# Modulation rows turned into columns: fp32 products with a vector of ones, or one-pass transposes and a VectorE sum

## The chip, the cores and the metric

The kernel runs on one core of a Trainium2 chip. Its time is the device time of one execution in microseconds (us). The kernel before took 1846.21 us (median of three runs, 1843.55 to 1846.67).

## The reference

Two layers, each a token mixer (layer 0: chunked gated linear attention, GLA; layer 1: an S5 state-space layer) around a residual stream of 256 tokens by 2048 features, everything in fp32. Ahead of each mixer the input is modulated by shift and scale vectors that a conditioning vector `c` gives:

```
mod = silu(c) @ ada_w + ada_b                      # per layer: 2048 -> 3 * 2048
for i in range(2):
    shift, scale, gate = split(mod[i], 3)          # 2048 each
    u = x * (1 + scale) + shift
    h = gla_mixer(u, ...) if i == 0 else s5_mixer(u, ...)
    x = layer_norm(alpha * x + (1 + gate) * h, ln_g[i], ln_b[i])
```

Only the way in which `shift` and `scale` get from the sums of products to the place where `u` is made is touched here.

## The kernel before

**Layout.** The mixers take `u` transposed: features on the 128 partitions, tokens along the free axis, in 16 blocks of 128 features. So `shift` and `scale` are wanted as columns: a tile `mods` of 128 partitions by (layer, part, block), part 0 the shift, part 1 one plus the scale. The products `silu(c) @ ada_w`, though, are gathered as rows: a tile of 128 partitions by up to 512 output features, in which each partition holds the part of the sum that its rows of `ada_w` gave, so that the total is still to be summed over the partitions. `mod_cols` does both steps at once: for each block of 128 features it multiplies the row block (as the stationary operand) with one column of ones, and the result is a column of 128 totals. VectorE then adds the bias `abT` (and 1.0 for the scale) and writes `mods`.

**Who makes the rows.** Layer 0's rows come from `ada_pe`, either by TensorE into a PSUM tile `psa` that ScalarE copies to `row` (L275, L278), or, with `dve=True`, by VectorE multiply-adds into `row` (L265, L267). Layer 1's come from `ada_dve`, by VectorE multiply-adds into `acc` (L311, L315), 512 features at a time. In all `mod_cols` is called 18 times: for layer 0 four times with two blocks and six times with four, for layer 1 eight times with four: 64 blocks in all. In the profile its products are line L236 (tile `psmod`), the bias adds L239 (shift) and L241 (scale).

**The work around it.** The weights of the big products stream in by DMA, 128 x 1024 at a time (`wload`, L136, issued by SyncE's queue); `split` makes of each a rounded part on ScalarE (`hi...`, L145) and a remainder on VectorE (`lo...`, L146), and TensorE multiplies with both (L167 to L169 for the v products and the output projection, L180 to L182 for q, k and z). `u` itself is made block by block: TensorE transposes x (`u_tr`, L363, tile `psx`), VectorE applies scale and shift (`u_fin`, L370, tile `uf`), and ScalarE and VectorE split that too (L351, L352). VectorE also adds the v products to `vbig` (L401) and scales the q and k products into `qk` (L415).

**Order.** Layer 0's modulation runs among the first 60 weight steps: a table (`put_ada`, `put_u`) says at which step a load, a product or the columns are put, and `issue_after` ties them to that step's last split and last matmul. Layer 1's steps wait in a list `bg` from which `pump` takes some at each weight step. Within these ties a scheduler sets each engine's order; every engine runs its own list in order. PSUM tiles of `mod_cols` come from the pool `ax` of three.

Of the kernel before, what the change touches and what calls it, by code (L numbers as in the profile page):

```python
# [8 lines left out]
F32 = mybir.dt.float32  # L9
F32R = mybir.dt.float32r  # L10
AF = mybir.ActivationFunctionType
ALU = mybir.AluOpType
# [3 lines left out]
P = 128  # L16
# [17 lines left out]
def trunk(ctx, tc, x, c, ln_g, ln_b, ada_w, ada_b, gla_w_in, gla_gate_w2, gla_gate_b, gla_norm_g,  # L34
# [3 lines left out]
    V, S, PE = nc.vector, nc.scalar, nc.tensor  # L38
# [3 lines left out]
    def pool(name, bufs=1, **kw):  # L42
        return ctx.enter_context(tc.tile_pool(name=name, bufs=bufs, **kw))

    cp = pool("const")
# [23 lines left out]
    ones = rp.tile([P, P], F32, tag="ones", name="ones0")  # L69
# [10 lines left out]
    def psx(name):  # L80
        return ax.tile([P, 512], F32, tag="ax", name=name)

    ident = cp.tile([P, P], F32, name="ident")
# [139 lines left out]
    ps = psx("psc")  # L223
# [6 lines left out]
    mods = cp.tile([P, 2, 2, 16], F32, name="mods")  # L230

    def mod_cols(row, l, part, k0, nk):

        ps = psx(f"psmod{l}{part}{k0}")
        for i in range(nk):
            PE.matmul(ps[:, i:i + 1], lhsT=row[:, i * P:(i + 1) * P], rhs=ones[:, 0:1], start=True, stop=True)  # L236
        ab = abT[:, 32 * l + 16 * part + k0:32 * l + 16 * part + k0 + nk]
        if part == 0:
            V.tensor_tensor(mods[:, l, 0, k0:k0 + nk], ps[:, 0:nk], ab, op=ALU.add)  # L239
        else:  # L240
            V.scalar_tensor_tensor(mods[:, l, 1, k0:k0 + nk], ps[:, 0:nk], 1.0, ab, op0=ALU.add, op1=ALU.add)  # L241

    def ada_pe(l, part, k0, nk, dve=False, rows=None):

# [37 lines left out]
        if dve:  # L282
            steps = [lambda kq=kq, h=h: madds(kq, h) for kq in range(len(rows)) for h in range(2)]
        return [lambda kq=kq: load(kq) for kq in range(len(rows))], steps, lambda: mod_cols(acc[0], l, part, k0, nk)

    def ada_now(*a, rows=None, between=None):
# [11 lines left out]
    def ada_dve(l, part, j):  # L298
# [18 lines left out]
        def fin():  # L317
            if part < 2:
                mod_cols(acc[0], l, part, 4 * j, 4)
            else:  # L320
                br = rp.tile([1, 512], F32, tag="br", name=f"br{l}{j}", bufs=1)
                dma(br, ada_b[l:l + 1, 2 * D + j * 512:2 * D + (j + 1) * 512])
                ps = psx(f"psg{l}{j}")
                V.tensor_tensor(acc[0][0:1, :], acc[0][0:1, :], br, op=ALU.add)
                if l:
                    ah = tp.tile([P, 512], F32R, tag="ah", name=f"ah{j}", bufs=1)
                    al = tp.tile([P, 512], F32R, tag="al", name=f"al{j}", bufs=1)
                    hilo(ah, al, acc[0])
                    PE.matmul(ps, lhsT=ones_r, rhs=ah, start=True, stop=False)
                    PE.matmul(ps, lhsT=ones_r, rhs=al, start=False, stop=True)  # L330
                else:
                    PE.matmul(ps, lhsT=ones, rhs=acc[0], start=True, stop=True)
                if gate_dst[l] is None:
                    gate_dst[l] = s8t(f"gate{l}", [D])
                S.activation(gate_dst[l][:, j * 512:(j + 1) * 512], ps, AF.Identity, bias=ones[:, 0:1])
# [111 lines left out]
    ps = psx("psv2")  # L447
# [395 lines left out]
    for h in range(4):  # L843
        ps = psx(f"psst{h}")
        for cc, (r, a, b) in enumerate(((0, 0, 256), (64, 64, 256), (0, 256, 384), (64, 320, 384))):
            for t in range(2):
                PE.matmul(ps[r:r + 64, a:b], lhsT=kt[:, 2 * h + t, cc * 64:cc * 64 + 64], rhs=qs[cc][:, 2 * h + t, :],
                          start=(t == 0), stop=(t == 1))
# [62 lines left out]
    for g in range(8):  # L911
# [9 lines left out]
        for f in range(4):  # L921
            i = (g * 4 + f) % 8
# [103 lines left out]
    for k in range(16):  # L1026
        ps = psx(f"psn{k}")
# [242 lines left out]
    for g in range(8):  # L1270
# [7 lines left out]
        for f in range(4):  # L1278
            i = (g * 4 + f) % 8
# [27 lines left out]
    ones = rp.tile([P, P], F32, tag="ones", name="ones1")  # L1307
# [14 lines left out]
    for g in range(8):  # L1322
# [17 lines left out]
        for f in range(4):  # L1340
            i = g * 4 + f
# [78 lines left out]
    ps = psx("psnb")  # L1420
    PE.transpose(ps[:2, 0:P], nbs, ident)
    row = tp.tile([2, P], F32, tag="row2", name="row2", bufs=1)
# [31 lines left out]
```

## Time and profile before

| | |
|---|---|
| median of three runs | 1846.21 us (1843.55 to 1846.67) |
| profiled execution, own time | 1847.81 us |
| its span on the core | 1846.0 us |
| mean granted TensorE clock | 0.989 |
| TensorE busy | 1795.7 us, 97% |
| VectorE busy | 1401.8 us, 76% |
| ScalarE busy | 895.7 us, 49% |
| products of `mod_cols` (L236) | 128 records, 12.2 us to 752.5 us after the start |
| VectorE idle ahead of the bias adds (L239, L241) | 16.8 us and 12.9 us |

The profile is of one execution; its span is the time from the first to the last record, and the execution's own time is 1.8 us more. A record is one instruction as the engine ran it. PE is TensorE's matmuls, PEld its weight loads, DVE VectorE, ACT ScalarE, SPq SyncE's queue. In rows of the timeline the first number is the start in us, the second the duration; in brackets stands how long the engine had been idle, and what ended that.

### The profile page before, as it was taken

To read this page: it belongs to the slowest core of one execution; us is meant where nothing else is said; L and a number is where in the kernel's file an instruction comes from. 1 tells how busy PE (TensorE), PEld (TensorE's weight loads), DVE (VectorE), ACT (ScalarE), POOL (GpSimd) and SP (SyncE) were. 2 spreads that over 40 slices of the span, in tenths; PEclk is the share of its full clock that TensorE was granted. 3 is DMA by queue.
4 is the path that set the end of the run, shared out by engine and by line. 5 is a ranking of instruction groups with operands and counts; after the bars stand their busy time and mean duration, and the time that the engine had idled before them with its cause. 6 is when DMAs were issued, how large, how long until landed. Compare 5 with 4: busy or idle time off the path is not lost.

```text
span 1846.0 us, 33780 instructions
## 1 busy us (share of the span) xinstructions
PE 1795.7 (97%) x13555; PEld 1587.8 (86%) x13555; DVE 1401.8 (76%) x1862; ACT 895.7 (49%) x1266; POOL 85.6 (5%) x94
## 2 busy tenths in 40 slices
PE   7999999999999999999999999999999999999997
PEld 5776897899999888799998989989888888888885
DVE  4877667879989988686799779888677775557556
ACT  4432557555556333554454444545544544444332
POOL 0000000000000000002232300000000000000000
PEclk9999999999999999999999999999999999999998
DMA  9996885889889998577666567899788886668653
GB/s 342 380 325 226 293 263 165 262 270 322 290 277 324 331 356 287 171 248 212 197 175 196 173 194 219 232 254 240 220 276 267 270 277 209 190 192 325 193 183 92
DMA packets 246101, 457.86 MB, mean 248 GB/s; under 512 B 19828, under 2 KB 49198, under 8 KB 244662
## 3 DMA queue, kind: packets, MB, share of 16 engines
q1 hardware_dynamic: 239320, 436.02, 73.8%
q0 software_dynamic: 5856, 18.63, 3.1%
q8 instruction: 106, 1.74, 0.4%
q10 hardware_dynamic: 768, 1.05, 0.2%
q14 instruction: 51, 0.42, 0.1%
HBM read 437.01 MB, written 18.61 MB: 247 GB/s over the span
## 4 chain that ended last, share of the span: by engine, by line
PE 83%; DVE 9%; DMA 3%; issue 2%; ACT 2%; POOL 0%; SPq 0%; DVEq 0%; ACTq 0%; POOLq 0%
PE gl L192 13%; PE gl L193 7%; PE op L168 6%; PE op L167 6%; PE op L169 6%; PE z L182 3%; PE z L180 3%; PE z L181 3%; PE v L168 3%; PE v L169 3%; PE v L167 3%; PE su L180 2%; PE su L181 2%; PE su L182 2%; PE sz L180 2%
## 5 line engine op out<-in xcount | busy, mean ns | idle before, releaser
L146 DVE TENSOR_TENSOR logl<-wgl,higl 128x1024 fp32r<-128x1024 f32 x128 | 156.6, 1223 | 115.7 <-ACT higl L145 109.2
L145 ACT CAST higl<-wgl 128x1024 fp32r<-128x1024 f32 x128 | 134.4, 1050 | 170.7 <-PE gl L192 163.0
L192 PE MATMUL gl<-yp,higl 128*128 128x512 f32 x512 | 179.3, 395 | 0.1
L192 PE MATMUL gl<-yb,higl 128*128 128x512 f32 x512 | 179.1, 395 | 0.0
L145 ACT CAST hio<-wo 128x1024 fp32r<-128x1024 f32 x95 | 100.2, 1055 | 154.7 <-PE op L169 134.4
L146 DVE TENSOR_TENSOR loo<-wo,hio 128x1024 fp32r<-128x1024 f32 x95 | 116.1, 1223 | 67.1 <-ACT hio L145 66.6
L315 DVE SCALAR_TENSOR_TENSOR acc<-wa,cs,acc 128x512 f32<-128x512 f32 x217 | 162.1, 747 | 4.0 <-DMA wa<-in_ada_w 1.1
L180 PE MATMUL sz<-u1h,hisz 128*128 128x256 f32 x512 | 151.0, 295 | 1.3 <-ACT zs L1282 1.2
L180 PE MATMUL su<-u1h,hisu 128*128 128x256 f32 x512 | 151.8, 298 | 0.0
L180 PE MATMUL z<-u0h,hiz 128*128 128x256 f32 x512 | 148.7, 290 | 0.0
L182 PE MATMUL sz<-u1h,losz 128*128 128x256 f32 x512 | 145.6, 285 | 3.1 <-DVE losz L146 3.1
L182 PE MATMUL su<-u1h,losu 128*128 128x256 f32 x512 | 146.7, 287 | 0.0
L181 PE MATMUL su<-u1l,hisu 128*128 128x256 f32 x512 | 146.4, 286 | 0.0
L182 PE MATMUL z<-u0h,loz 128*128 128x256 f32 x512 | 144.9, 283 | 0.6 <-DVE loz L146 0.6
L181 PE MATMUL sz<-u1l,hisz 128*128 128x256 f32 x512 | 145.4, 284 | 0.0
L181 PE MATMUL z<-u0l,hiz 128*128 128x256 f32 x512 | 144.7, 283 | 0.0
L193 PE MATMUL gl<-yb,logl 128*128 128x256 f32 x512 | 142.9, 279 | 0.0
L193 PE MATMUL gl<-yp,logl 128*128 128x256 f32 x512 | 142.2, 279 | 0.0
L145 ACT CAST hisz<-wsz 128x1024 fp32r<-128x1024 f32 x64 | 67.0, 1050 | 117.7 <-PE sz L181 62.0
L192 PEld LDWEIGHTS gl<-yp,higl 128*128 128x128 f32 x512 | 95.9, 188 | 22.8 <-issue 0.7
L192 PEld LDWEIGHTS gl<-yb,higl 128*128 128x128 f32 x512 | 96.0, 188 | 22.6
L168 PE MATMUL v<-lov,u0h 128*128 128x512 f32 x256 | 103.6, 406 | 6.9 <-DVE lov L146 6.8
(321 smaller groups left out, 4974.0 us busy)
## 6 DMA issues: line engine op xcount, KB each, us to landing
wgl<-in_s_w_glu SPq DMA_DIRECT2D x128, 512.0 KB, 4.5
wa<-in_ada_w SPq DMA_DIRECT2D x116, 512.0 KB, 5.3
wv<-in_gla_w_in SPq DMA_DIRECT2D x64, 512.0 KB, 5.8
wz<-in_gla_w_in SPq DMA_DIRECT2D x64, 512.0 KB, 5.1
wsu<-in_s_w_in SPq DMA_DIRECT2D x64, 512.0 KB, 4.3
wsz<-in_s_w_in SPq DMA_DIRECT2D x64, 512.0 KB, 5.7
wo<-in_s_w_out SPq DMA_DIRECT2D x64, 512.0 KB, 4.6
a<-in_ada_w SPq DMA_DIRECT2D x31, 1024.0 KB, 10.8
```

The source lines that it names most:

```text
L145: S.copy(hi, w)
L146: last_lo[0] = V.tensor_tensor(lo, w, hi.bitcast(F32), op=ALU.subtract).ins
L167: PE.matmul(banks[tt], lhsT=uh, rhs=hi[:, kk, :], start=(k == first), stop=False)
L168: PE.matmul(banks[tt], lhsT=uh, rhs=lo[:, kk, :], start=False, stop=False)
L169: last_mm[0] = PE.matmul(banks[tt], lhsT=ul, rhs=hi[:, kk, :], start=False, stop=(k == last)).ins
L180: PE.matmul(o, lhsT=wh, rhs=u.hi(k), start=(k == first), stop=False)
L181: PE.matmul(o, lhsT=wh, rhs=u.lo(k), start=False, stop=False)
L182: last_mm[0] = PE.matmul(o, lhsT=wl, rhs=u.hi(k), start=False, stop=(k == last)).ins
L192: PE.matmul(banks[f], lhsT=hi[:, kk, fs], rhs=u.both(k), start=(k == 0), stop=False)
L193: PE.matmul(banks[f][:, :T], lhsT=lo[:, kk, fs], rhs=u.hi(k), start=False, stop=(k == last))
L315: V.scalar_tensor_tensor(acc[0], w[:, kk, :], cs[:, k:k + 1], acc[0], op0=ALU.mult, op1=ALU.add)
```

## The change

`mod_cols` no longer multiplies with ones. It transposes each row block on TensorE, into a PSUM tile of 128 x (blocks x 128) in which partition p holds, for each block, the 128 addends of feature p; VectorE sums them along the free axis into a small tile `modsum`; the bias adds then read `modsum` in place of PSUM.

```
     ps = psx(f"psmod{l}{part}{k0}")
     for i in range(nk):
-        PE.matmul(ps[:, i:i + 1], lhsT=row[:, i * P:(i + 1) * P], rhs=ones[:, 0:1], start=True, stop=True)
+        PE.transpose(ps[:, i * P:(i + 1) * P], row[:, i * P:(i + 1) * P], ident)
+    sm = cp.tile([P, 4], F32, tag="modsum", name=f"modsum{l}{part}{k0}", bufs=2)[:, :nk]
+    V.tensor_reduce(sm, ps[:, :nk * P].rearrange("p (i q) -> p i q", i=nk), op=ALU.add, axis=mybir.AxisListType.X)
     ab = abT[:, 32 * l + 16 * part + k0:32 * l + 16 * part + k0 + nk]
     if part == 0:
-        V.tensor_tensor(mods[:, l, 0, k0:k0 + nk], ps[:, 0:nk], ab, op=ALU.add)
+        V.tensor_tensor(mods[:, l, 0, k0:k0 + nk], sm, ab, op=ALU.add)
     else:
-        V.scalar_tensor_tensor(mods[:, l, 1, k0:k0 + nk], ps[:, 0:nk], 1.0, ab, op0=ALU.add, op1=ALU.add)
+        V.scalar_tensor_tensor(mods[:, l, 1, k0:k0 + nk], sm, 1.0, ab, op0=ALU.add, op1=ALU.add)
```

All later line numbers grow by two. TensorE's instructions stay as many, apart from one group of layer 1 that the scheduler now splits in one and three; VectorE's grow by 18. The scheduler also moves some neighbours. Two places matter for what follows, both on VectorE in layer 0; names carry the buffer's number, and what is the same tile has a number greater by 10 to 12 in the changed kernel.

VectorE about 83 us after the start, before, at the scale of blocks 4 to 7 (`vbig` is the running sum of the v products, `lov` the remainder of the next weights, which TensorE needs):

```order
L267 SCALAR_TENSOR_TENSOR row_527<-a_525,cs,row_527 128x512
L401 TENSOR_TENSOR vbig<-vbig,v_761 128x512
L241 SCALAR_TENSOR_TENSOR mods<-psmod_751,abT 128x4
L401 TENSOR_TENSOR vbig<-vbig,v_762 128x512
L146 TENSOR_TENSOR lov_788<-wv_651,hiv_787 128x1024
L146 TENSOR_TENSOR lov_819<-wv_677,hiv_818 128x1024
L401 TENSOR_TENSOR vbig<-vbig,v_785 128x512
```

The same place in the changed kernel:

```order
L269 SCALAR_TENSOR_TENSOR row_535<-a_533,cs,row_535 128x512
L403 TENSOR_TENSOR vbig<-vbig,v_771 128x512
L146 TENSOR_TENSOR lov_798<-wv_659,hiv_797 128x1024
L238 TENSOR_REDUCE modsum_764<-psmod_759 128x4
L403 TENSOR_TENSOR vbig<-vbig,v_772 128x512
L243 SCALAR_TENSOR_TENSOR mods<-modsum_764,abT 128x4
L146 TENSOR_TENSOR lov_829<-wv_685,hiv_828 128x1024
L403 TENSOR_TENSOR vbig<-vbig,v_795 128x512
```

The first `lov` has moved ahead of everything that waits for `psmod`; the reduce and the bias add stand behind it, with a `vbig` between them.

VectorE about 101 us after the start, before, at the shift of blocks 4 to 7 (`loq` is the remainder of the next q weights, `uf` the modulated input, from which the next stationary blocks are made):

```order
L415 SCALAR_TENSOR_TENSOR qk_115<-q_934,qk_115 128x256
L146 TENSOR_TENSOR loq_992<-wq_783,hiq_991 128x1024
L239 TENSOR_TENSOR mods<-psmod_924,abT 128x4
L415 SCALAR_TENSOR_TENSOR qk_115<-q_935,qk_115 128x256
L415 SCALAR_TENSOR_TENSOR qk_115<-q_936,qk_115 128x256
L415 SCALAR_TENSOR_TENSOR qk_115<-q_937,qk_115 128x256
L370 TENSOR_SCALAR uf_975<-psx_970,mods 128x256
```

The same place in the changed kernel:

```order
L417 SCALAR_TENSOR_TENSOR qk_115<-q_946,qk_115 128x256
L238 TENSOR_REDUCE modsum_939<-psmod_934 128x4
L146 TENSOR_TENSOR loq_1004<-wq_793,hiq_1003 128x1024
L241 TENSOR_TENSOR mods<-modsum_939,abT 128x4
L417 SCALAR_TENSOR_TENSOR qk_115<-q_947,qk_115 128x256
L417 SCALAR_TENSOR_TENSOR qk_115<-q_948,qk_115 128x256
L417 SCALAR_TENSOR_TENSOR qk_115<-q_949,qk_115 128x256
L372 TENSOR_SCALAR uf_987<-psx_982,mods 128x256
```

Here the reduce has gone in ahead of `loq`, and nothing else has changed its place.

## The prediction

> **What bounds the kernel now.** I read the busy times first, then the chain of work that ended last, then the stretches of the span in which the columns are made.
>
> ```profile
> PE 1795.7 (97%) x13555; PEld 1587.8 (86%) x13555; DVE 1401.8 (76%) x1862; ACT 895.7 (49%) x1266; POOL 85.6 (5%) x94
> PE 83%; DVE 9%; DMA 3%; issue 2%; ACT 2%; POOL 0%; SPq 0%; DVEq 0%; ACTq 0%; POOLq 0%
> ```
>
> TensorE is busy for 97% of the span and carries 83% of the chain, so a microsecond of TensorE work is usually a microsecond of time. Usually is not everywhere, so I look at the windows in which the 18 groups lie. The columns are the stretch, then busy time and instructions of PE, PEld, DVE, ACT and POOL, the granted clock, the DMA share and GB/s.
>
> ```profile
> 60.00:110.00 50.00, 45.17 (x269) 37.04 (x270) 42.97 (x69) 19.53 (x29) 0.00 (x0) 0.97 1.00 358
> 510.00:590.00 80.00, 80.00 (x641) 78.79 (x641) 71.97 (x86) 47.77 (x69) 0.00 (x0) 1.00 0.90 305
> 590.00:755.00 165.00, 164.85 (x744) 136.04 (x743) 142.72 (x173) 65.62 (x65) 0.00 (x0) 1.00 0.89 302
> ```
>
> Around the late eight groups (layer 1, 520 to 752 us) TensorE never stops: 80.00 of 80 us and 164.85 of 165. VectorE has 8.03 and 22.28 us free there. Up to 110 us it is different: TensorE is idle for 4.83 of 50 us, VectorE busy for 42.97, and the DMA engines are full (1.00). There, a shorter product need not end anything sooner.
>
> **What is removed and added on TensorE.** The grouped records give the old product and the nearest relative of the new one, the transposes of x.
>
> ```profile
> L236 PE MATMUL psmod<-ones,row 128*128 128x1 f32 x64 | 8.9, 256 | 0.7 <-ACT row L278 0.7
> L236 PE MATMUL psmod<-ones,acc 128*128 128x1 f32 x64 | 7.6, 239 | 0.0
> L363 PE MATMUL psx<-ident,xrow 128*128 128x128 f32 x32 | 5.1, 292 | 0.0
> ```
>
> The 64 blocks took 128 records, two passes for each product; the 32 transposes of x took 32, one pass each. A mean of one overlaps its neighbours, so I take no difference of means, but the slot in a running stream. Two groups stand 3 us apart among the same q products:
>
> ```profile
> 183.54 0.28 PE L181 MATMUL q<-u0l,hiq 128*128 128x256 f32 x1
> 183.66 0.95 PE L236 MATMUL psmod<-ones,row 128*128 128x1 f32 x8
> 184.47 0.36 PE L182 MATMUL q<-u0h,loq 128*128 128x256 f32 x1
> 184.64 0.16 DVE L239 TENSOR_TENSOR mods<-psmod,abT 128x4 f32<-128x4 f32 x1 [2.23 <-PE psmod L236]
> 184.67 0.28 PE L180 MATMUL q<-u0h,hiq 128*128 128x256 f32 x1
> ...
> 186.34 0.28 PE L182 MATMUL q<-u0h,loq 128*128 128x256 f32 x1
> 186.46 0.60 PE L363 MATMUL psx<-ident,xrow 128*128 128x128 f32 x4
> 186.82 0.36 PE L180 MATMUL q<-u0h,hiq 128*128 128x256 f32 x1
> 187.02 0.28 PE L181 MATMUL q<-u0l,hiq 128*128 128x256 f32 x1
> ```
>
> The last q product ahead of the ones starts at 183.54, the last one ahead of the transposes at 186.34. From there to the second q product behind, where the stream has its pace again, it is 184.67 - 183.54 = 1.13 us with four blocks of ones and 187.02 - 186.34 = 0.68 us with four transposes. A group of four saves 0.45 us. For 14 such groups that is 6.3 us; two groups of two at 44 and 52 us would add 0.22 each. The first two groups of two (12 and 18 us) stand before waits and get a reduce into a chain that VectorE waits for, so I set them at nothing:
>
> ```profile
> 16.66 0.23 PEld L275 LDWEIGHTS psa<-a,cz 128*32 128x32 f32 x8 [0.63 <-DMA a<-in_ada_w]
> 19.31 0.16 DVE L241 SCALAR_TENSOR_TENSOR mods<-psmod,abT 128x2 f32<-128x2 f32 x1 [5.80 <-PE psmod L236]
> ```
>
> (In the timeline's rows the bracket is the idle time before, and what ended it.) Behind the first group, TensorE waits at 16.66 for a load of `a` that comes no sooner; behind the second, `uf` starts right after 19.31, and two transposes with a reduce take about what the old products took. The ceiling of the gain is 6.7 us.
>
> **What is added on VectorE.** 18 reduces, from PSUM: 14 over 512 elements of a partition, 4 over 256. No reduce of this form is in the trace. The nearest rows:
>
> ```profile
> L947 DVE BATCH_NORM_STATS2 st<-big 128x6 f32<-128x512 f32 x16 | 11.0, 687 | 0.1
> L370 DVE TENSOR_SCALAR uf<-psx,mods 128x256 f32<-128x256 f32 x16 | 7.9, 538 | 2.4 <-PE psx L363 2.3
> L239 DVE TENSOR_TENSOR mods<-psmod,abT 128x4 f32<-128x4 f32 x7 | 1.1, 160 | 4.0 <-PE psmod L236 4.0
> ```
>
> The statistics also take in 512 elements and put out a few: 0.69 us. The other end is `uf`, which reads 256 from PSUM in 0.54 us: twice that is 1.08. I take 0.69, the row of the same width and kind; a reduce of 256 gets 0.42, what a 256-wide pass costs at 103.22 below. Together 14 x 0.69 + 4 x 0.42 = 11.3 us more on VectorE (15.1 to 17.3 by the other end). The bias add stays at 0.16: it reads a small tile instead of PSUM. So the change moves work from the full engine to the one with 444 us free, and what counts is whether the reduce fits at its place.
>
> [...]
>
> **The late eight groups.** Each reduce and bias add stand among the splits that TensorE needs.
>
> ```profile
> 523.66 1.22 DVE L146 TENSOR_TENSOR loz<-wz,hiz 128x1024 fp32r<-128x1024 f32 x1
> 527.35 1.06 ACT L145 CAST hiz<-wz 128x1024 fp32r<-128x1024 f32 x1 [1.82 <-PE z L181]
> 622.22 1.05 ACT L145 CAST hio<-wo 128x1024 fp32r<-128x1024 f32 x1 [4.31 <-DMA wo<-in_gla_w_out]
> 634.99 0.19 PEld L168 LDWEIGHTS op<-loo,hy 128*128 128x128 f32 x1 [0.47 <-DVE loo L146]
> 761.11 0.69 DVE L941 TENSOR_TENSOR ot<-op,gate 128x512 f32<-128x512 f32 x1 [3.13 <-PE op L169]
> ```
>
> At the first of them VectorE has finished `loz` at 524.88, and the rounded part two steps on is started at 527.35 only because TensorE has then given its buffer back: VectorE is 2.47 us ahead. The reduce and the 0.45 us by which TensorE comes sooner take 1.14 of that. Where the last group ends, VectorE still waits 3.13 us for TensorE. So the reduces are covered and TensorE's saving is time, as long as the weights come. They do, with one exception: at 622.22 ScalarE has waited 4.31 us for `wo` while the residual is loaded, and TensorE then runs dry (0.47 us at 634.99), so the group ahead of it (617 us) only waits longer there. Seven groups x 0.45 = 3.2 us. Bounds: 0, if the transfers (0.89 to 0.90 of all DMA time) set the pace, to 3.6, if all eight count.
>
> **Four groups at 126 to 205 us.** They stand in stretches of q and v products where VectorE waited for TensorE (2.23 us ahead of the bias add at 184.64, for one). 4 x 0.45 = 1.8 us, with 0 as the low end if the v products' `lov` is late anyway, as in the rows on the clock below.
>
> **The groups up to 110 us.** Two things meet here. At 83 us the first `lov` moves ahead of all that waits for `psmod`:
>
> ```profile
> 83.21 0.16 DVE L241 SCALAR_TENSOR_TENSOR mods<-psmod,abT 128x4 f32<-128x4 f32 x1 [0.93 <-PE psmod L236]
> 84.16 2.35 DVE L146 TENSOR_TENSOR lov<-wv,hiv 128x1024 fp32r<-128x1024 f32 x2
> 85.43 0.50 PE L168 MATMUL v<-lov,u0h 128*128 128x512 f32 x1 [1.21 <-DVE lov L146]
> ...
> 98.49 0.13 PEld L275 LDWEIGHTS psa<-a,cz 128*32 128x32 f32 x4 [0.30 <-DMA a<-in_ada_w]
> ...
> 103.22 0.42 DVE L415 SCALAR_TENSOR_TENSOR qk<-q,qk 128x256 f32<-128x256 f32 x1 [0.29 <-PE q L182]
> 103.94 0.42 DVE L415 SCALAR_TENSOR_TENSOR qk<-q,qk 128x256 f32<-128x256 f32 x1 [0.30 <-PE q L182]
> ```
>
> TensorE's wait of 1.21 us for `lov` at 85.43 goes, and four groups save up to 1.35 us (two of four blocks, two of two). But at 98.49 the stream waits for a load with all DMA engines full, so whoever comes there earlier than 0.30 us waits instead: what was won before 98 us mostly ends there. At 101 us the reduce goes in ahead of `loq`, where VectorE is short: it has 0.29 + 0.30 = 0.59 us of idle time before `uf`, against 0.69 for the reduce, so `uf` comes 0.10 us later if nothing else shifts. Kept: 0.30 - 0.10 = 0.2 us. Bounds: -0.7 (the reduce wholly unhidden, nothing won) to +2.6 (all of 1.35 and 1.21).
>
> **The sum.** 0.2 + 1.8 + 3.2 = 5.2 us less. The sum stands against the profiled execution (span 1846.0, own time 1847.81, 1.6 above the median of the runs); I apply it to the median: 1846.2 - 5.2 = 1841.0. A measurement of this kernel tells about 0.2% from no change, 3.7 us: faster is below 1842.5, slower above 1849.9.
>
> **Rivals.** *The clock falls once more* (1842.7). Some waits of TensorE are followed by a few microseconds at half the granted clock, others are not:
>
> ```profile
> 158.31 0.63 PE L168 MATMUL v<-lov,u0h 128*128 128x512 f32 x1 [1.88 <-DVE lov L146]
> 158.00:160.00 2.00, 1.69 (x4) 1.32 (x5) 1.64 (x5) 0.00 (x0) 0.00 (x0) 0.63 0.88 240
> 160.00:162.00 2.00, 2.00 (x6) 1.59 (x5) 1.31 (x3) 0.00 (x0) 0.00 (x0) 0.51 1.05 397
> ...
> 109.67 0.73 PE L167 MATMUL v<-hiv,u0h 128*128 128x512 f32 x2 [1.56 <-ACT hiv L145]
> 108.00:110.00 2.00, 0.44 (x2) 0.30 (x2) 1.98 (x4) 1.66 (x3) 0.00 (x0) 1.00 0.77 248
> ```
>
> The wait of 1.88 us at 158.31 cost (1 - 0.63) x 2 + (1 - 0.51) x 2 = 1.7 us of clock; that of 1.56 at 109.67 cost none (the clock is 1.00). The wait at 109.67 is for VectorE's and ScalarE's chain. If TensorE gets there up to 0.4 us sooner and the chain no sooner, it becomes about 2 us, and 1.7 us go back: 1842.7. Against it: only the longer waits fell. [...]
>
> *The saving is absorbed* (1844.2). If the transfers set the late stage, its 3.2 us are given back at the waits for `wo`, and only 0.2 + 1.8 stay; much the same if a transpose of these rows took two passes. For it: DMA at 0.90. Against it: TensorE's 80.00 of 80.
>
> *All of it counts* (1838.3): 6.7 and 1.2 us. Against it stand the waits for loads at 16.66 and 98.49.
>
> *VectorE becomes the bound at the late groups* (1851.8, slower). Its place is the `lo` parts between 520 and 752 us: each reduce delays a `loz` or `loo` that TensorE then waits for, eight times 0.69 us, and TensorE's saving shows nowhere: 1846.2 + 5.6. It decides once VectorE's lead is under 1.14 us instead of 2.47, or a reduce takes over 2 us. VectorE's 71.97 of 80 us speaks for it, the lead at 524.88 against it.
>
> **How the numbers follow.** Likeliest, 45%: 1841.0, by itself 1839.5 to 1842.4. Clock, 25%: 1842.7, on either side of 1842.5. Absorbed, 13%: 1844.2. All counts, 10%: 1838.3. VectorE bound, 7%: 1851.8. Faster is the first, the fourth and a small part of the second: 0.60; within 0.2%: 0.33; slower: 0.07. The range 1838 to 1846 leaves out the slower rival and the tails.
>
> **What the changed kernel's profile would show.** `psmod` with 64 records, and among q products a slot of 0.68 us in place of 1.13; if 128, the saving is gone. Reduces at 0.69 us (0.54 to 1.08). VectorE still waiting ahead of most of them, and TensorE full from 510 to 590 us; a PE wait there for `loz` or `loo` would prove the slower rival. The wait at 85.43 gone, and more time at the load of `a` near 98 us. A granted clock near 0.5 at 110 to 114 us would show the clock's rival; a longer wait for `wo` near 622 us the lost eighth group. What would make it wrong: reduces over 2 us, waits early in layer 0 that shift the clock elsewhere, or weights that come just in time.

## The result, and the profile after

The changed kernel took 1836.32 us (median of five, 1834.65 to 1839.11) beside 1846.21 us (five runs, 1843.55 to 1847.54): a ratio of 0.9946, interval 0.9934 to 0.9958. That is 9.9 us less, where 5.2 were forecast, and below the low end of the range (1838.0). One later execution of the kernel before took 2500.78 us at a granted clock of 0.654 and is left out of every mean. The profiled execution has a span of 1837.1 us. Its busy times, and the windows in which the columns are made (moved to where the same work now lies):

```profile
PE 1781.8 (97%) x13491; PEld 1574.5 (86%) x13491; DVE 1410.3 (77%) x1880; ACT 895.4 (49%) x1266; POOL 88.0 (5%) x94
60.00:110.00 50.00, 46.12 (x276) 36.58 (x280) 45.43 (x72) 18.98 (x29) 0.00 (x0) 1.00 1.02 365
503.00:583.00 80.00, 80.00 (x637) 78.63 (x636) 74.25 (x90) 48.28 (x69) 0.00 (x0) 1.00 0.89 310
583.00:746.00 163.00, 162.48 (x723) 133.36 (x723) 145.25 (x176) 65.16 (x64) 0.00 (x0) 1.00 0.89 306
```

TensorE has 64 records fewer, VectorE 18 more, and TensorE is still nearly full in the late stretches (80.00 of 80 us, 162.48 of 163). The groups of instructions give the prices:

```profile
L236 PE MATMUL psmod<-ident,row 128*128 128x128 f32 x32 | 5.6, 289 | 1.1 <-ACT row L280 0.7 <-DVE row L269 0.4
L236 PE MATMUL psmod<-ident,acc 128*128 128x128 f32 x32 | 5.0, 272 | 0.0
L238 DVE TENSOR_REDUCE modsum<-psmod 128x4 f32<-128x512 f32 x14 | 9.7, 694 | 4.0 <-PE psmod L236 4.0
L238 DVE TENSOR_REDUCE modsum<-psmod 128x2 f32<-128x256 f32 x4 | 1.7, 425 | 17.2 <-PE psmod L236 17.2
```

The 64 blocks now take 64 records, one each, and the reduces take 0.694 and 0.425 us (0.69 and 0.42 were taken). The group among the q products, whose slot was 1.13 us:

```profile
177.66 0.28 PE L182 MATMUL q<-u0h,loq 128*128 128x256 f32 x1
177.78 0.62 PE L236 MATMUL psmod<-ident,row 128*128 128x128 f32 x4
178.16 0.36 PE L180 MATMUL q<-u0h,hiq 128*128 128x256 f32 x1
178.36 0.28 PE L181 MATMUL q<-u0l,hiq 128*128 128x256 f32 x1
```

From the last q product ahead to the second behind it is 0.70 us (0.68 was taken).

**Where the time went, stretch by stretch.** A weight split on ScalarE (L145) marks the same point of the work in every kernel. Two such points in the timelines, first before, then after:

```profile
507.47 1.05 ACT L145 CAST hiz<-wz 128x1024 fp32r<-128x1024 f32 x1
763.88 1.05 ACT L145 CAST hisu<-wsu 128x1024 fp32r<-128x1024 f32 x1
```

```profile
500.84 1.05 ACT L145 CAST hiz<-wz 128x1024 fp32r<-128x1024 f32 x1
754.05 1.05 ACT L145 CAST hisu<-wsu 128x1024 fp32r<-128x1024 f32 x1
```

The lead is 6.63 us at the first and 9.83 at the second: 3.2 us were won between them. The table does this with eleven points, so for twelve stretches, and for six profiles; the other profiles are given below where they matter. Its first columns are the stretch and its length in the first profile of before; the others are the difference to that; in brackets stand the microseconds of the stretch at half granted clock. "Again" is another execution of the same kernel.

```
 stretch       before      before     early only  changed    changed    late only
                           again                             again
   0.0-  44.9  44.91( 0.0) -0.73(3.4) -1.80(3.4) -0.29(6.8) -0.50(6.8) -1.67(3.4)
  44.9-  60.4  15.47( 0.0) -0.00(0.0) -0.28(0.0) -0.27(0.0) -0.28(0.0) -0.01(0.0)
  60.4-  92.4  32.02( 3.4) -0.03(3.4) -1.90(3.4) -2.05(0.0) -2.05(0.0) -0.03(3.4)
  92.4- 117.8  25.41( 0.0) +0.01(0.0) -0.42(0.0) -0.43(0.0) -0.45(0.0) +0.01(0.0)
 117.8- 141.7  23.89( 0.0) +0.00(0.0) -0.33(0.0) -0.33(0.0) -0.33(0.0) +0.05(0.0)
 141.7- 172.6  30.94( 6.8) -3.06(0.0) -0.82(6.8) -2.28(3.4) -2.25(3.4) -1.45(3.4)
 172.6- 231.6  59.01( 0.0) -0.02(0.0) -0.95(0.0) -0.93(0.0) -0.94(0.0) -0.00(0.0)
 231.6- 507.5 275.82( 0.0) -0.01(0.0) -0.01(0.0) -0.03(0.0) -0.01(0.0) -0.03(0.0)
 507.5- 577.0  69.57( 0.0) +0.00(0.0) +0.00(0.0) -0.91(0.0) -0.91(0.0) -0.91(0.0)
 577.0- 763.9 186.84( 0.0) -0.01(0.0) +0.01(0.0) -2.30(0.0) -1.79(0.0) -2.35(0.0)
 763.9-1306.2 542.37(17.1) -0.33(13.7) -0.83(6.8) +1.12(10.2) -0.31(17.1) -6.06(6.8)
1306.2-1846.0 539.79(11.6) -0.22(11.5) +0.54(10.2) -0.27(11.7) +0.15(11.2) +0.11(12.0)
```

Between 45 and 577 us, stretches without a change of the clock repeat to some hundredths of a microsecond, so single effects can be read there; from 577.0 to 763.9 us the two profiles of the changed kernel differ by 0.51. Three things cannot be read so: the start, the stretches in which the clock falls (141.7 to 172.6), and the stretch from 764 to 1306 us, which varies by several microseconds although no instruction of `mod_cols` lies in it. Much of that comes between 960 and 1107 us (times of the first profile of before), where TensorE's waits of over 0.15 us add up to 8.96 us in the first profile of before, 5.56 in late only, and 7.2 to 7.7 in the other four. The one that differs most, first before, then late only (us in total, times, longest):

```profile
PE sz L182 <- DVE losz L146: 3.1, 1, 3.1
```

```profile
PE sz L182 <- DVE losz L146: 1.3, 1, 1.3
```

### The profile page after: what moved, and what is told of

The parts are those of the page before. It is cut to its first block, busy times and chain, and to the rows that moved or that the text cites. A ratio compares the mean times of both kernels' runs of the same rounds, so it can differ in the third digit from the quotient of the medians.

```text
span 1837.1 us, 33664 instructions
## 1 busy us (share of the span) xinstructions
PE 1781.8 (97%) x13491; PEld 1574.5 (86%) x13491; DVE 1410.3 (77%) x1880; ACT 895.4 (49%) x1266; POOL 88.0 (5%) x94
## 4 chain that ended last, share of the span: by engine, by line
PE 78%; DVE 11%; DMA 4%; issue 3%; ACT 2%; POOL 0%; SPq 0%; DVEq 0%; ACTq 0%; POOLq 0%
PE gl L192 13%; PE gl L193 7%; PE op L168 6%; PE op L169 6%; PE op L167 6%; PE z L182 3%; PE z L181 3%; PE z L180 3%; PE v L168 3%; PE v L169 2%; PE v L167 2%; PE su L180 2%; PE su L181 2%; PE su L182 2%; PE sz L180 2%
## 5 line engine op out<-in xcount | busy, mean ns | idle before, releaser
L145 ACT CAST higl<-wgl 128x1024 fp32r<-128x1024 f32 x128 | 134.4, 1051 | 172.4 <-PE gl L192 167.5
L145 ACT CAST hio<-wo 128x1024 fp32r<-128x1024 f32 x95 | 100.2, 1055 | 152.8 <-PE op L169 131.9
L145 ACT CAST hisz<-wsz 128x1024 fp32r<-128x1024 f32 x64 | 67.0, 1049 | 113.6 <-PE sz L181 57.4
L145 ACT CAST hiz<-wz 128x1024 fp32r<-128x1024 f32 x64 | 67.2, 1051 | 88.2 <-PE z L181 80.8
```

The costliest lines, as they stand in the source:

```text
L145: S.copy(hi, w)
```

## The experiments

The edits below are abridged to what differs. "Equal clock" means that both profiles compared have the same number of falls in the stretch.

**Halves of the change.** Two kernels with the new form in one layer only:

```
-    (all calls of mod_cols: transposes, reduce)
+    if l == 1:      # "late only";  l == 0 in "early only"
+        transposes, reduce, bias add from modsum
+    else:
+        products with ones, bias add from PSUM
```

> Transposes and reduces for the eight groups of layer 1 alone; layer 0 keeps the products with ones, and every engine's order there is that of before. Theory (TensorE's saved passes are the gain): 0.45 us for each of eight groups, of which one is lost where wo is late, so 3.2 us less than before (1843.0), and nothing changes ahead of 510 us. Rival (the change mostly pays through layer 0, by the order on VectorE and the waits that the clock follows): the same 3.2 us here, but then the greater part, over 5 us, must come from the other half. Rival (later waits in layer 1 shift with the start): more than 3.2 us although nothing changed early.

> Transposes and reduces for the ten groups of layer 0 alone; layer 1 keeps the products with ones. Every engine's order up to 500 us is that of the changed kernel. Theory as forecast: 2.0 us less than before. What the two profiles suggest instead: 6.6 us less up to 240 us, of which about 1.8 us are the four groups at 126 to 205 us, 1.4 us the stretch up to 110 us, and 3.4 us two stretches of half clock that did not come; if these come again in this run, 3.0 to 3.5 us less; if their absence is a lasting effect of the change, 6 to 7 us less in the median.

Late only: 1836.37 us (ratio 0.9952, interval 0.9934 to 0.9970); its late stretches are 0.91 + 2.35 = 3.3 us shorter, as the theory has it, and layer 0 gives nothing outside the clock. These 3.3 us do not explain its time: alone they would be a ratio of 0.9982, above the interval. In its profile, 12.3 us shorter than the first of before, the rest is the start, the clock and the stretch from 764 us (-6.06). Its six executions have a mean granted clock of 0.9928, against 0.9908 in 84 of before, and 0.0020 of 1841 us is 3.7 us at most. The changed kernel has the same late form and a clock of 0.9911, so this may be the luck of six executions, but that is not shown, and some 2 us of the 9 stay open.

Early only: 1838.29 us (0.9961, 0.9943 to 0.9980). It has the same falls of the clock between 45 and 232 us as the first profile of before, which makes the comparison clean: 0.28 + 1.90 + 0.42 + 0.33 + 0.82 + 0.95 = 4.7 us less, not 2.0. Alone that would be a ratio of 0.9975, within the interval. It is also more than the 3.0 to 3.5 that I had expected if the falls came again. I had taken off 1.7 us for each of two falls, and the one at 61 to 63 us costs next to nothing: the stretch from 60 to 92 us is 1.90 us shorter here with a fall, and 2.05 in the changed kernel without one.

**The same kernels again, for the clock.** No edit.

> The kernel before once more, for its clock. Theory (a fall of the clock behind a wait is a matter of where the wait lies in time, and so of chance): in this profile the waits of 2.34, 1.88 and 1.79 us at 62, 158 and 165 us are there again, but not all three are followed by a half clock; the places of the falls differ from those of the first profile. Rival (the falls belong to these waits): half clock at 63, 158 and 165 us again. The time is 1846 in both.

> The changed kernel once more, for its clock. Theory (chance): the waits of 2.34 us at 61.5 and 1.91 us at 154 and 159 us are there again, and one or more of the first two may now be followed by half clock, with 1.7 us each; the sum of the gains without the clock is the same (3.2 us between 505 and 755 us). Rival (lasting): again a single fall, at 159.7. The median is about 9.9 us under before.

The kernel before took 1844.28 us, the changed kernel 1836.82 (0.9952, 0.9935 to 0.9970). In the new profile of before both waits for `lov` are there, and neither is followed by half clock:

```profile
157.56 0.50 PE L168 MATMUL v<-lov,u0h 128*128 128x512 f32 x1 [1.89 <-DVE lov L146]
162.50 0.50 PE L168 MATMUL v<-lov,u0h 128*128 128x512 f32 x1 [1.92 <-DVE lov L146]
159.00:162.00 3.00, 1.58 (x7) 0.95 (x6) 2.98 (x6) 1.05 (x1) 0.00 (x0) 1.00 1.01 362
162.00:165.00 3.00, 2.50 (x11) 2.09 (x12) 3.00 (x5) 0.00 (x0) 0.00 (x0) 1.00 0.54 203
```

The stretch is 3.06 us shorter with the same program, 1.5 us for each fall. In the changed kernel, in both profiles, the wait of 1.91 us at 154 is not followed by a fall, that at 159 is, and none comes at 61 (in the first profile the clock is 1.00 from 154 to 158 us, 0.50 for 3.41 us from 159.68, and 1.00 from 61 to 66); so far this is what the rival had (lasting). But early only and the kernel with four reduces (below), whose instructions of layer 0 are those of the changed kernel, do have a fall there, at 60.95 and 61.30 us. So the falls by which the first pair of profiles differed come and go with the same instructions, and I count them as chance and no part of the change. Over 84 executions of before and 11 of the changed kernel the mean granted clock was 0.9908 and 0.9911: 0.0003 of 1841 us, some 0.6 us.

**All but the group at 83 us, and that group alone.**

```
-    if True:                                    # new form everywhere
+    if not (l == 0 and part == 1 and k0 == 4):  # "all but"; without the not: "alone"
```

> The changed kernel, but the group at 83 us (scale of blocks 4 to 7, layer 0) keeps its products with ones; with that the bias add stands ahead of the first lov again, as before. Theory (the passes saved there and the lov that no longer stands behind the bias add are worth the whole 1.45 to 1.66 us, and the loads of a behind it absorb nothing): between 60 and 92 us the stretch is as long as before at equal clock, 1.5 to 2.0 us longer than in the changed kernel, and the wait of about 1.2 us for lov near 84 us is back; all other stretches are those of the changed kernel. Rival (my forecast: the full DMA engines take it back): the stretch up to 118 us ends at the same place as in the changed kernel, within 0.3 us.

> Before, with the one group at 83 us by transposes and a reduce; 17 groups keep their products with ones. lov stands ahead of the reduce there, as in the changed kernel. Theory (the move of lov and one group's passes): from 60 to 92 us 1.9 us less than before at equal clock, from 92 to 118 us nothing taken back by the loads (0 to 0.1 us), and no change behind; 1843 to 1844 in the mean. Rival (my forecast): the loads of a take back all but 0.3 us by 118 us.

"All but": without the new form in this group the bias add stands ahead of `lov` again, and the wait is back:

```profile
82.25 0.16 DVE L252 SCALAR_TENSOR_TENSOR mods<-psmod,abT 128x4 f32<-128x4 f32 x1 [0.85 <-PE psmod L247]
83.20 2.35 DVE L146 TENSOR_TENSOR lov<-wv,hiv 128x1024 fp32r<-128x1024 f32 x2
84.48 0.79 PE L168 MATMUL v<-lov,u0h 128*128 128x512 f32 x1 [1.21 <-DVE lov L146]
84.00:86.00 2.00, 1.52 (x4) 1.23 (x5) 1.56 (x2) 0.00 (x0) 0.00 (x0) 0.61 1.05 387
86.00:88.00 2.00, 2.00 (x7) 1.57 (x6) 0.69 (x1) 0.00 (x0) 0.00 (x0) 0.53 1.04 368
```

This time the clock fell behind it. The stretch from 60 to 92 us is 1.40 us longer than before with 3.4 us of half clock in each, 0.5 us longer by 118 us; 1838.44 us in all (0.9955, 0.9941 to 0.9969). Beside the changed kernel, which has no fall there, it is 3.0 us longer by 118 us; with 1.5 us for the fall, an estimate from the pair of profiles above, 1.5 us are left for the group, the low end of what was expected.

The group alone gives 1.98 us less from 60 to 92 us at equal clock, then +0.08 by 118 us and +0.27 by 142 us: the loads take nothing back to speak of, and my rival falls. Its time, 1843.32 (0.9990, 0.9977 to 1.0002), is 2.3 us under before, as far as such a difference can be told.

**Transposes without the sum.**

```
-    V.tensor_reduce(sm, ps..., op=ALU.add, axis=X)
+    sm = ps[:, :nk * P] as (p, i, q), element q = 0
```

> Transposes as in the changed kernel, but without the reduces: the bias add reads one addend of each feature from PSUM, so the sum over the partitions is left out. lov stands ahead of the bias add at 83 us, as in the changed kernel. Theory (the reduces are hidden): the same stretches as in the changed kernel, to 0.1 us: 0.91 us less than before from 507 to 577 us, 2.3 less up to 764 us, 0.43 less from 92 to 118 us, and the time of the changed kernel within its spread (1836.5). Rival (a reduce costs where VectorE is short): 0.1 to 0.7 us shorter at each of the groups up to 205 us, above all at 101 us, up to 3 us in all.

1836.87 us (0.9943, 0.9922 to 0.9964), from 1829.84 to 1838.05. At equal clock, 45 to 232 us give 5.4 us less than before instead of 4.7; 507.5 to 577.0 us give the same 0.91, and 577.0 to 763.9 give 2.93 instead of 2.30. So the reduces cost some 0.7 us in layer 0 and 0.6 in the late groups; in the time of the whole kernel this does not show. In layer 0 the stretch from 92 to 118 us is 1.93 us shorter than before instead of 0.42, but 0.9 of these 1.5 us come back by 173 us. In the late groups the changed kernel has a short wait that neither before nor this kernel has:

```profile
590.20 0.50 PE L168 MATMUL op<-loo,hy 128*128 128x512 f32 x1 [0.41 <-DVE loo L146]
```

**An ordinary product with the identity.**

```
-    PE.transpose(ps[:, i * P:(i + 1) * P], row[:, i * P:(i + 1) * P], ident)
+    PE.matmul(ps[:, i * P:(i + 1) * P], lhsT=row[:, i * P:(i + 1) * P], rhs=ident, ...)
```

> The same columns by an ordinary fp32 product with the identity in place of the transposes; reduce and bias add as in the changed kernel. The price of such a product is in no trace here: a product with one column has two passes of 0.12 us, and 128 columns cannot be cheaper. Theory (TensorE's time in the slot counts one for one where TensorE never stops): two records a product, a slot among the q products of 1.13 us or more, and the stretch from 507 to 577 us is longer than before by twice (slot - 1.13). Rival (what pays is the order on VectorE and not the passes): the stretches stay as in the changed kernel, 0.91 us under before from 507 to 577 us.

```profile
L236 PE MATMUL psmod<-ident,row 128*128 128x128 f32 x64 | 9.8, 293 | 0.9 <-ACT row L280 0.7 <-DVE row L269 0.2
L236 PE MATMUL psmod<-ident,acc 128*128 128x128 f32 x64 | 8.6, 274 | 0.0
```

Two records a product, as with ones. From 507.5 to 577.0 us it takes what before took (+0.00; the theory had it 0.14 longer), from 577.0 to 763.9 0.23 less; so all but 0.23 of the late gain is the saved pass. From 60 to 92 us, though, 1.57 of the 1.90 us are there without any pass saved, and from 92 to 118 us 0.38 of the 0.42: `lov` stands ahead of the reduce, and TensorE has no wait over 0.3 us from 60 to 92 us but the one at 61. 1843.91 us in all (0.9990, 0.9976 to 1.0004).

The same output took two records by the product and one by the transpose, and four of them moved the stream by 0.70 instead of 1.20 us (from the q product at 178.30 to the second behind at 179.50): half the records and 0.58 of the time, in what this stream sees.

**Ones, and a copy.**

```
-    mods = bias add from ps
+    V.tensor_copy(sm, ps[:, :nk]);  mods = bias add from sm
```

> Products with ones as before, and VectorE copies their result into the small tile, from which the bias adds read: 18 instructions more on VectorE, nothing saved on TensorE, order on TensorE and SyncE that of before, lov still behind the bias add at 83 us. Theory: nothing changes in any stretch but those with the clock, 1845 in the mean. Rival (reading the bias add from SBUF and giving PSUM back sooner is part of the gain): more than 1 us less up to 240 us at equal clock.

1844.55 us (0.9996, 0.9979 to 1.0013). All stretches from 45 to 764 us are within 0.1 us of before, apart from +0.28 from 172.6 to 231.6. An SBUF source for the bias add gained nothing here.

**Four reduces in place of one, in layer 1.**

```
-    V.tensor_reduce(sm, ...)
+    for _ in range(4 if l == 1 else 1): V.tensor_reduce(sm, ...)
```

> The changed kernel with each reduce of layer 1 done four times (the same result written again), which puts 3 x 0.69 us more on VectorE at each of the eight groups, among the splits. Layer 0 is that of the changed kernel. Theory (VectorE has 8 us free of 80 at the first groups and 22 of 165 behind, and a lead of 2.5 us): 507 to 577 us still 0.9 us less than before, 577 to 764 us 1.5 to 2.3 us less. Rival (VectorE is near to being the bound there, as my slower case had it): each further reduce costs its 0.69 us, and the stretch from 507 to 764 us is up to 16 us longer than in the changed kernel.

1839.81 us (0.9969, 0.9957 to 0.9981). Neither was right. From 507.5 to 577.0 us it is 1.90 us longer than the changed kernel, from 577.0 to 763.9 2.78: 4.7 us for 24 reduces of 0.69 us, so a good quarter of 16.6 us shows.

```profile
527.84 0.39 PE L182 MATMUL z<-u0h,loz 128*128 128x256 f32 x1 [0.56 <-DVE loz L146]
532.35 0.39 PE L182 MATMUL z<-u0h,loz 128*128 128x256 f32 x1 [0.68 <-DVE loz L146]
```

TensorE now waits for `loz` at the first group. VectorE's lead covers one reduce and not four. The lead of 2.47 us at 524.88, from the trace of before, gives about the size: one reduce and TensorE's earlier arrival take 1.14, three more reduces 3 x 0.69, together 3.2, so some 0.7 us of wait by this estimate; the rows show 0.56 and 0.68. Here 8 us free in 80 were no cover for the 3 x 0.69 us that had to be done within the next two steps.

## Why the prediction was wrong

**The late eight groups: right in size, half right in reason.** 3.2 us were forecast and 3.2 measured (0.91 + 2.30), in three of four profiles with the new form and the reduce there; the fourth gave 2.7. Seven groups of 0.455 us count. One does not, but in these three not because `wo` was late: ScalarE waits 3.68 to 4.77 us for it near 615 us, and 4.31 and 3.35 in the two profiles of before. The lead shrinks at 590 us, where TensorE waits 0.41 us for `loo`; without the reduces that wait is gone and 3.8 us come. In the fourth profile `wo` did come later, with a wait of 5.68 us, and 0.5 us less was won. The changed kernel's first profile, then its second:

```profile
614.60 1.05 ACT L145 CAST hio<-wo 128x1024 fp32r<-128x1024 f32 x1 [4.16 <-DMA wo<-in_gla_w_out]
```

```profile
615.89 1.05 ACT L145 CAST hio<-wo 128x1024 fp32r<-128x1024 f32 x1 [5.68 <-DMA wo<-in_gla_w_out]
```

**The four groups at 126 to 205 us: 1.8 forecast, 2.1 measured** at equal clock (0.33 + 0.82 + 0.95).

**The groups up to 110 us: the step that failed.** "Kept: 0.30 - 0.10 = 0.2 us" measured 0.28 + 1.90 + 0.42 = 2.6 us, the upper bound that I had worked out and set aside. Two readings were wrong. First, I took the 0.30 us at 98.49 for a wait that would absorb what was won. The row behind it in the trace of before shows the same gap without a load, and the matmuls (PE) run through:

```profile
98.03 1.92 PE L275 MATMUL psa<-a,cz 128*32 128x512 f32 x16
98.49 0.13 PEld L275 LDWEIGHTS psa<-a,cz 128*32 128x32 f32 x4 [0.30 <-DMA a<-in_ada_w]
98.92 0.13 PEld L275 LDWEIGHTS psa<-a,cz 128*32 128x32 f32 x4 [0.30 <-issue]
```

0.30 us is the gap ahead of these weight loads where no transfer ends it too (98.92 above, 95.88 and 96.31 below); the landing of `a` only happened to be the last event named. In the changed kernel, 2.6 us earlier, nothing waits for the load, and the matmuls take the same 1.92 us:

```profile
95.42 1.92 PE L277 MATMUL psa<-a,cz 128*32 128x512 f32 x16
95.42 0.16 PEld L277 LDWEIGHTS psa<-a,cz 128*32 128x32 f32 x8
95.88 0.13 PEld L277 LDWEIGHTS psa<-a,cz 128*32 128x32 f32 x4 [0.30 <-issue]
96.31 0.13 PEld L277 LDWEIGHTS psa<-a,cz 128*32 128x32 f32 x4 [0.30 <-issue]
```

The DMA share of 1.00 said here that the transfers were busy, not that anyone waited for them. So the 1.21 us ahead of `lov` went for good, by the move of `lov` alone, as the identity product shows:

```profile
81.51 0.60 PE L236 MATMUL psmod<-ident,row 128*128 128x128 f32 x4
81.55 1.23 DVE L146 TENSOR_TENSOR lov<-wv,hiv 128x1024 fp32r<-128x1024 f32 x1
82.68 0.69 DVE L238 TENSOR_REDUCE modsum<-psmod 128x4 f32<-128x512 f32 x1
82.88 0.45 PE L168 MATMUL v<-lov,u0h 128*128 128x512 f32 x1
```

Second, the reduce at 101 us did not make that stretch longer than before, though without the reduces it is shorter still. It went in ahead of `loq`, and the three q scalings behind, which had waited for TensorE one by one, ran together:

```profile
99.36 1.22 DVE L146 TENSOR_TENSOR loq<-wq,hiq 128x1024 fp32r<-128x1024 f32 x1
100.49 0.16 DVE L241 TENSOR_TENSOR mods<-modsum,abT 128x4 f32<-128x4 f32 x1
100.56 1.08 DVE L417 SCALAR_TENSOR_TENSOR qk<-q,qk 128x256 f32<-128x256 f32 x3
```

**The sum** of the direct effects at equal clock is 2.6 + 2.1 + 3.2 = 7.9 us, not 5.2; of these 2.7 us more, 2.4 are the step above. By itself that would have been 1838.3 us, at the low end of the range. The rest is not of a known cause: the first pair of medians is 9.9 us apart, but the means of 84 later executions of before (1845.5 us) and 11 of the changed kernel (1836.7) are 8.9 apart, with 95% between 7.7 and 10.1. The remaining 1.0 is within that; the clock's mean would give 0.6 of it, and the start and the stretch from 764 to 1306 us could give as much to either side. What makes the waits in that stretch vary was not settled. Late only, 9 us faster with 3.3 us of direct effects, shows that a sum and a time can differ by far more, so that the agreement here proves little.

**The rivals.** "All of it counts" (10%) came nearest, and its 1838.3 was still above the measured time. That its 6.7 + 1.2 us equal the 7.9 of the direct effects is in part luck: a late group did not count, and up to 118 us the order gave 1.57 + 0.38 us with no pass saved, where the rival had 1.2. Absorption and VectorE as the bound did not come, though four reduces show where the latter begins (that rival's 5.6 us should read 8 x 0.69 = 5.5). The clock did not fall at the wait behind 109.67 (now 1.55 us at 106.63) in any profile, not even with the group at 83 us alone, where that wait grew to 2.00 us at 107.33. But I had treated the falls behind the waits at 62, 158 and 165 us as fixed parts of the kernel, and the same program has one of them in one profile and all three in another.

**Chances.** The range was drawn around a sum whose largest unknown, -0.7 to +2.6 us up to 110 us, I had put near the lower end on the strength of one row; with its upper end, 2.4 us more, in the range, the low end would have been 1838 - 2.4 = 1835.6.

## What to carry to other kernels

A wait that a row names may be taken for a wait for that event only if the same gap is missing where that event is not: look at the neighbours of the same form before a gap of a few tenths is made the reason that a gain is lost. A change that adds an instruction can pay by what the scheduler then puts ahead of it: here moving one weight remainder ahead of a small operation that waits for TensorE was worth 1.6 us, more than the saved passes of three groups (3 x 0.455). To find effects of half a microsecond in 1846, compare the start of the same instruction in two traces, stretch by stretch, and hold the granted clock of both beside it.

## What the runs showed of the hardware

Up to 232 us the granted clock of the first pair of profiles fell to half for 3.41 us, or twice that, 0.9 us or less from the end of a wait of TensorE: before at 62.96, 158.53 and 165.36 us, at the waits of 2.34, 1.88 and 1.79 us that end at 62.06, 158.31 and 164.71; in the changed kernel at 19.73 and 159.68 us, at those of 1.73 and 1.91 us that end at 20.07 and 159.06. In all but the group at 83 us it fell at a wait of 1.21 us (ending at 84.48; clock 0.61 from 84 to 86 us), while the waits of 2.34 us at 61.50 and 1.91 us at 154.09 in the changed kernel were followed by none. At the same wait it fell in one execution and not in another; one fall cost 1.5 us where TensorE was the bound (3.06 us for two, from 141.7 to 172.6 us). The falls of each of these two profiles start whole multiples of 3.413 us apart, the length of one fall: before, the 95.57 us from the first to the second are 28 times that and the 6.83 us from there to the third twice that; in the changed kernel, the 139.95 us are 41 times that. The four falls of the one and the three of the other in the stretch from 764 to 1306 us lie on the same steps. What decides at which wait the clock falls was not shown. Where VectorE was next in line a fall cost little: from 60 to 92 us the changed kernel is as long without a fall (-2.05) as the early-only kernel with one (-1.90), because without the fall TensorE comes sooner and waits, among others 0.64 us for `lov` at 76.84, where the first profile of before, with a fall, shows none from 66 to 80 us:

```profile
76.84 0.50 PE L168 MATMUL v<-lov,u0h 128*128 128x512 f32 x1 [0.64 <-DVE lov L146]
```
